# Delta-rule chunks of a two-block diffusion transformer: the identity of the Newton residual moves from TensorE's accumulation to VectorE's eviction, and the last chunk's directions are summed on VectorE

## The chip, the cores and the metric

The kernel runs on one core of a Trainium2 chip. A time is the device time of one execution in microseconds (us). A core has five instruction queues that run side by side and wait for each other through semaphores: PE (TensorE, matmuls; its weight loads are listed as PEld), DVE (VectorE), ACT (ScalarE), POOL (GpSimd) and SP (SyncE, here the queue that issues most transfers). Each queue runs its instructions strictly in the order in which the program has them. Matmuls write to PSUM, which is read by DVE and ACT; everything else lies in SBUF.

## The reference

One launch computes two transformer blocks on 512 tokens of width 1024. Block 1 has two recurrences side by side (HGRN2 and a gated delta rule, each with 4 heads of 128, in both directions of time, each started from a context of 256 tokens), an output projection and a mixture of 16 experts; block 2 has attention, a gating unit and two convolutional feed-forward layers. The change touches the delta rule:

```
a_mat = where(strict, beta * (k k^T) * decay, 0) + eye      # per chunk and head, unit lower triangular
sol   = triangular_solve(a_mat, [k*beta*exp(cum), v*beta])  # w, u
v_new = u - w @ state
o     = q_dec @ state + (q k^T * decay) @ v_new
state = g_tot * state + k_dec^T @ v_new
...
return oc_f + flip(oc_b), ox_f + flip(ox_b)                 # the two directions are summed
```

The kernel uses chunks of 128 tokens: 2 of the context and 4 of the sequence, in each of two directions, so 12 chunks.

## The kernel before, in words

The program is written with a tile library: pools of buffers, and one list of instructions in which waits are put in by the library, and in which the order on each engine is chosen by the library's scheduler when the program is built. So a changed instruction can move others.

Of the whole program the delta-rule core takes the stretch from about 472 to 690 us. `dn_core` makes 12 generators (`dn_chunk`, one for each chunk and direction) and `in_turn(chunks, 5, 3, fill)` runs them: up to five chunks are in flight, a new one enters every third turn, and each `yield` ends a chunk's turn. `fill` adds the steps of a matrix-vector product (block 2's modulation) while it lasts. I call three turns a round: one chunk enters and one leaves in each.

A chunk goes through these steps, all on tiles of 128 x 512 (4 heads side by side):

- lines 1035 to 1041: the decays, `r` and `a` (on GpSimd, in the context's chunks on VectorE), cumulated by matmuls, and `e`, their exponential, on ScalarE.
- lines 1051, 1052: `a *= e`, `a *= kk` on VectorE; then `a` is transposed into `at`, and half-precision inverses `xi` and `ti` are begun (1061 to 1066; the masked copy into `ti` is line 1065).
- lines 1067 to 1088: six levels of block doubling. Each multiplies `at` with `ti` into `y` (evicted by ScalarE, 1072), `y` with `xi` and `xi` with `y`, and copies both products under a mask into `xi` and `ti` (VectorE, 1086 and 1087; the last two levels copy blocks, 1029).
- lines 1089 to 1098: two Newton steps on the inverse, `xf += tb^T (I + a^T xf)`, where `a` is by then the negated matrix with its diagonal. The residual `I + a^T xf` is made in a PSUM bank, evicted as the bfloat16 tile `res`, and multiplied with `tb`; line 1098 adds the product to `xf` on VectorE. This is the place of the first edit.
- lines 1102 to 1146: the read-out matrix `qk`, `vb` (line 1117, VectorE, 4 small instructions), `vn`, the output `o` (ScalarE, 1132; VectorE, 1133) and the new state (VectorE, 1145). For the second direction to reach a chunk, `finish` is given: its output goes to `dnoc`, is added to the first direction's in `dno` (line 1135), and is normed and gated by `head_out` (ScalarE line 787, VectorE 305, GpSimd 306, VectorE 790). This is the place of the second edit.

PSUM gives the chunks a pool `mm` of 5 banks and a pool `aux` of 3.

After the core follows block 1's output projection: its weights come by SP (line 506) into `wraw` and `wrawx`, ScalarE rounds them into `whi` (line 270), VectorE takes the remainder `wlo` (line 273), the gated outputs are transposed on PE (650) and split into `hhi` and `hlo` in the same way, and three matmuls (530 to 532) make one product. `hosq` is the scratch tile of `head_out`'s squares.

Of the kernel before, what the change touches and what calls it, by code (L numbers as in the profile page):

```python
# [225 lines left out]
class Kern:  # L226
# [771 lines left out]
    def dn_chunk(self, pool, d, c, x, ab, s, po, finish=None, zero=False, last=False):  # L998
# [6 lines left out]
        nc = self.nc  # L1005
        inc, exc = self.incs[d], self.c["lt" if d else "gt"]
        d4 = slice(4 * d, 4 * d + 4)
        full, hb = [P, 4, P], lambda ap: ap.unsqueeze(2).to_broadcast([P, 4, P])
# [7 lines left out]
        def mm4(p, l, r, start=True, stop=True):  # L1016
            for h in range(4):
                nc.tensor.matmul(p[:, h, :], l[:, h, :], r[:, h, :], start=start, stop=stop)
# [13 lines left out]
        p = aux()  # L1032
# [7 lines left out]
        a = tile_("a")  # L1040
        eng.tensor_mul(a, exc.unsqueeze(1).to_broadcast(full), hb(ab["nbeta"][:, c, d4]))
        yield
        if ("kk", c) not in x:
            for n, l in (("kk", "kT"), ("qk", "qT")):
                if l in x:
                    p = mmt()
# [7 lines left out]
        p = aux()  # L1054
# [12 lines left out]
        for l in range(5, -1, -1):  # L1067
            yield
            p = aux()
# [7 lines left out]
            if l == 0:  # L1077
                xf, tb = tile_("xf"), tile_("tb", BF16)
# [9 lines left out]
        for i in range(2):  # L1088
            yield
            p = mmt()  # L1090
            nc.tensor.matmul(p, self.identb, self.identb.unsqueeze(1).to_broadcast(full), start=True, stop=False)
            for h in range(4):
                nc.tensor.matmul(p[:, h, :], a[:, h, :], xf[:, h, :], start=False, stop=h == 3)
            res = tile_("res", BF16)
            nc.scalar.copy(res, p)
            p = mmt()
            mm4(p, tb, res)
            nc.vector.tensor_add(xf, xf, p)

        yield  # L1100
        if po is not None:
            nc.gpsimd.tensor_mul(e, e, x["qk", c][d])
            p = aux()
# [9 lines left out]
        if not zero:  # L1113
            p = mmt()
# [5 lines left out]
        p = mmt()  # L1120
# [4 lines left out]
        if po is not None:  # L1125
            p = mmt()
            mm4(p, x["qT"][:, :, cs], s)
            p2 = mmt()
            mm4(p2, qk, vn)
            o = tile_("oc")  # L1130
            for h in range(4):
                nc.scalar.mul(o[:, h, :], p[:, h, :], ab["ec"][:, c, 4 * d + h:4 * d + h + 1])
            nc.vector.tensor_add(o if finish else po, o, p2)
            if finish:
                nc.gpsimd.tensor_add(po, po, o)
                finish()
        if last:
            return
        p = mmt()
# [974 lines left out]
```

## Time and profile before

| | |
|---|---|
| median of three runs | 2383.46 us (2381.67 to 2384.58) |
| the profiled execution | 2387.35 us |
| its span, first to last instruction | 2385.5 us |
| PE busy over the span | 94% |
| DVE busy | 68% |
| ACT busy | 50% |
| POOL busy | 26% |
| mean granted clock of TensorE | 0.972 of full speed |

The busy shares are means over stages with different limits. A stage is read from its own stretch of the trace.

### The profile page before, as it was taken

What the parts mean: (1) busy time and instruction counts of PE and PEld (TensorE: products, weight loads), DVE (VectorE), ACT (ScalarE), POOL (GpSimd) and SP (SyncE); (2) the same over time, 40 slices, a digit from 0 to 9 for tenths busy, and PEclk for the clock granted to TensorE, in tenths of its full rate; (3) what the DMA queues carried; (4) which work ended last, traced back from release to release, by engine and by line L of the source; (5) the groups of instructions that cost most, each with busy time, mean ns of one, the idle gap of its engine ahead of it and who ended that gap; (6) DMA issues with size and microseconds to landing.
All of it is one profiled execution on the core that took longest, in us unless ns stands there. A gap on an engine that the chain in (4) does not pass through costs nothing.

```text
span 2385.5 us, 33834 instructions
## 1 busy us (share of the span) xinstructions
PE 2240.5 (94%) x13058; PEld 1880.5 (79%) x13058; DVE 1614.3 (68%) x2545; ACT 1200.8 (50%) x1969; POOL 620.3 (26%) x470
## 2 busy tenths in 40 slices
PE   6998989989988899999999999999999999999998
PEld 3988977758875677778778878878888988888887
DVE  4777877778855888886857865896673445553553
ACT  4455644456754677776337763432342433432433
POOL 2133544345421111100441422332333001110111
PEclk9999999999999899999999999999999999999999
DMA  8564004151045799997210002656433222323321
GB/s 317 186 222 143 28 1 153 46 219 74 2 177 230 281 395 368 372 379 267 77 39 1 2 36 107 237 193 231 148 131 102 102 89 71 106 73 113 106 74 60
DMA packets 68405, 355.24 MB, mean 149 GB/s; under 512 B 8065, under 2 KB 12817, under 8 KB 37009
## 3 DMA queue, kind: packets, MB, share of 16 engines
q1 hardware_dynamic: 62752, 333.94, 38.0%
q0 software_dynamic: 5488, 19.11, 3.3%
q8 instruction: 104, 1.70, 0.3%
q14 instruction: 61, 0.49, 0.1%
HBM read 334.45 MB, written 19.40 MB: 148 GB/s over the span
## 4 chain that ended last, share of the span: by engine, by line
PE 43%; DVE 5%; issue 1%; ACT 1%; DMA 0%; POOL 0%; SPq 0%; POOLq 0%; DVEq 0%; ACTq 0%
PE mm L531 12%; PE mm L532 12%; PE mm L530 12%; PE sc L1598 2%; PE av L1751 1%; PE aux L1616 1%; DVE mva L385 1%; PE av L1742 1%; DVE smax L1605 1%; DVE wlo L273 1%; PE aux L1587 0%; DVE cy L1868 0%; PE aux L388 0%; DVE st L1577 0%; DVE alo L273 0%
## 5 line engine op out<-in xcount | busy, mean ns | idle before, releaser
L530 PE MATMUL mm<-hhi,whi 128*128 128x512 f32 (+1 forms) x1184 | 438.0, 375 | 10.3 <-ACT whi L270 5.3
L531 PE MATMUL mm<-hlo,whi 128*128 128x512 f32 (+1 forms) x1184 | 441.5, 374 | 2.9 <-DVE hlo L482 2.9
L532 PE MATMUL mm<-hhi,wlo 128*128 128x512 f32 (+1 forms) x1184 | 438.7, 372 | 0.0
L270 ACT CAST whi<-wraw 128x1024 fp32r<-128x1024 f32 (+1 forms) x240 | 246.3, 1041 | 300.1 <-PE mm L531 223.5
L273 DVE TENSOR_TENSOR wlo<-wraw,whi 128x1024 fp32r<-128x1024 f32 (+1 forms) x203 | 249.3, 1244 | 179.9 <-ACT whi L270 179.1
L273 DVE TENSOR_TENSOR wlo<-wrawx,whi 128x1024 fp32r<-128x1024 f32 x190 | 229.0, 1230 | 94.3 <-ACT whi L270 93.0
L270 ACT CAST whi<-wrawx 128x1024 fp32r<-128x1024 f32 (+1 forms) x210 | 215.0, 1048 | 154.2 <-PE mm L531 106.1
L530 PEld LDWEIGHTS mm<-hhi,whi 128*128 128x128 f32 x1184 | 224.8, 191 | 49.4 <-ACT whi L270 5.9
L531 PEld LDWEIGHTS mm<-hlo,whi 128*128 128x128 f32 x1184 | 225.9, 191 | 41.5 <-DVE hlo L482 3.3
L532 PEld LDWEIGHTS mm<-hhi,wlo 128*128 128x128 f32 x1184 | 225.4, 191 | 38.0 <-issue 0.2
L530 PE MATMUL mm<-whi,hhi 128*128 128x512 f32 (+1 forms) x640 | 218.2, 346 | 6.3 <-ACT hhi L481 2.3
L532 PE MATMUL mm<-whi,hlo 128*128 128x512 f32 (+1 forms) x640 | 219.9, 347 | 3.8 <-DVE hlo L482 3.7
L531 PE MATMUL mm<-wlo,hhi 128*128 128x512 f32 (+1 forms) x640 | 219.6, 345 | 0.5 <-DVE wlo L273 0.4
L385 DVE SCALAR_TENSOR_TENSOR mva<-mvr,cc_c,mva 128x512 f32<-128x512 f32 x154 | 156.6, 1017 | 3.4 <-DMA mvr<-in_w_mod_dram 1.2
L1878 POOL TENSOR_TENSOR cy<-cy,csg 128x512 f32<-128x512 f32 x44 | 64.7, 1472 | 348.0 <-DVE cy L1870 332.5
L531 PE MATMUL mm<-alo,whi 128*128 128x512 f32 (+1 forms) x396 | 145.0, 366 | 0.0
L530 PE MATMUL mm<-ahi,whi 128*128 128x512 f32 (+1 forms) x396 | 144.7, 367 | 0.0
L532 PE MATMUL mm<-ahi,wlo 128*128 128x512 f32 (+1 forms) x396 | 144.4, 366 | 0.0
L273 POOL TENSOR_TENSOR wlo<-wraw,whi 128x1024 fp32r<-128x1024 f32 (+1 forms) x37 | 90.1, 2434 | 203.7 <-ACT whi L270 195.4
L530 PEld LDWEIGHTS mm<-whi,hhi 128*128 128x128 f32 x640 | 125.1, 196 | 20.3 <-ACT hhi L481 2.8
L532 PEld LDWEIGHTS mm<-whi,hlo 128*128 128x128 f32 x640 | 124.9, 196 | 19.7 <-DVE hlo L482 6.2
L531 PEld LDWEIGHTS mm<-wlo,hhi 128*128 128x128 f32 x640 | 125.0, 196 | 14.4 <-DVE wlo L273 1.3
(548 smaller groups left out, 4672.4 us busy)
## 6 DMA issues: line engine op xcount, KB each, us to landing
wrawx<-in_w_down_dram SPq DMA_DIRECT2D x32, 1024.0 KB, 9.1
wrawx<-in_w_gate_dram SPq DMA_DIRECT2D x30, 1024.0 KB, 9.0
wraw<-in_w_up_dram SPq DMA_DIRECT2D x30, 1024.0 KB, 9.2
wraw<-in_ffn_w_up_dram SPq DMA_DIRECT2D x30, 1024.0 KB, 4.8
mvr<-in_ada_w_dram SPq DMA_DIRECT2D x56, 512.0 KB, 4.5
wraw<-in_ada_w_dram SPq DMA_DIRECT2D x20, 1024.0 KB, 4.9
wraw<-in_w_in_dram SPq DMA_DIRECT2D x18, 1024.0 KB, 6.9
mvr<-in_w_mod_dram SPq DMA_DIRECT2D x32, 512.0 KB, 4.4
```

Source lines behind the costliest of these rows:

```text
L270: nc.scalar.copy(hi, src)
L273: (lo_eng or nc.vector).tensor_sub(lo, src, hi.bitcast(F32))
L385: nc.vector.scalar_tensor_tensor(acc, raw[:, k, :], c, acc, op0=ALU.mult, op1=ALU.add)
L530: nc.tensor.matmul(out, ahi, bhi, start=start, stop=False)
L531: nc.tensor.matmul(out, ahi, blo, start=False, stop=False)
L532: nc.tensor.matmul(out, alo, bhi, start=False, stop=stop)
L1598: nc.tensor.matmul(s[:, a:a + n], qs[:, qt * P:qt * P + P], ks[i][:, a:a + n], start=i == 0, stop=i == 1)
L1605: nc.vector.tensor_reduce(m, s[:, :768], axis=AX.X, op=ALU.max, negate=True)
L1616: nc.tensor.transpose(tp[:, j, :], p[:, (a + j) * P:(a + j + 1) * P], self.ident)
L1742: nc.tensor.matmul(av[:, qt, :], pt[:, k, :], hd["v"][:, k, :], start=k == 0, stop=k == 5)
L1751: nc.tensor.matmul(av[j * 64:j * 64 + 64, qt, :], hd["v"][:, k, :], pt[:, k, :], start=k == 0, stop=k == 5, tile_position=(0, j * 64))
L1878: nc.gpsimd.tensor_mul(y, y, sg)
```

## The change

Two edits. First, the identity: before, a bfloat16 matmul of the identity with itself puts `I` into the bank, four single-precision matmuls accumulate `a^T xf` onto it, and ScalarE casts the bank to `res`. After, the four matmuls start the bank, and VectorE's `tensor_add` reads the bank and the float32 identity (a constant in SBUF, repeated for the 4 heads) and writes `res`. That happens twice in each of 12 chunks. Second, where a chunk is the last of its direction (`last`, i == 3, which is so for the last two chunks of the 12), line 1135's sum of the two directions runs on VectorE and not on GpSimd.

```diff
         for i in range(2):
             yield
             p = mmt()
-            nc.tensor.matmul(p, self.identb, self.identb.unsqueeze(1).to_broadcast(full), start=True, stop=False)
-            for h in range(4):
-                nc.tensor.matmul(p[:, h, :], a[:, h, :], xf[:, h, :], start=False, stop=h == 3)
+            mm4(p, a, xf)
             res = tile_("res", BF16)
-            nc.scalar.copy(res, p)
+            nc.vector.tensor_add(res, p, self.ident.unsqueeze(1).to_broadcast(full))
             p = mmt()
             mm4(p, tb, res)
             nc.vector.tensor_add(xf, xf, p)
...
             if finish:
-                nc.gpsimd.tensor_add(po, po, o)
+                (nc.vector if last else nc.gpsimd).tensor_add(po, po, o)
                 finish()
```

The scheduler answers by moving neighbours. In the changed program line 1095's eviction is line 1093, 1098 is 1096, 1117 is 1115, 1133 is 1131 and 1135 is 1133; elsewhere in this text lines are those of the kernel before.

VectorE, one round in the middle of the core, before (`dnxf` is `xf`, `dnkkc` the chunk's k k^T, `smask` the masks):

```order
L1117 SCALAR_TENSOR_TENSOR dnvb<-mm,dnt,dnvb 128x128 x4
L1098 TENSOR_TENSOR dnxf<-dnxf,mm 128x512
L1086 COPY_PREDICATED dnxi<-smask,mm 128x512
L1087 COPY_PREDICATED dnti<-smask,mm 128x512
L1051 TENSOR_TENSOR dna<-dna,dne 128x512
L1086 COPY_PREDICATED dnxi<-smask,mm 128x512
L1087 COPY_PREDICATED dnti<-smask,mm 128x512
L1052 TENSOR_TENSOR dna<-dna,dnkkc 128x512
L1098 TENSOR_TENSOR dnxf<-dnxf,mm 128x512
L1065 COPY_PREDICATED dnti<-smask,dna 128x512
```

The same stretch of VectorE after the change (`cst` is the constant that holds the identity):

```order
L1115 SCALAR_TENSOR_TENSOR dnvb<-mm,dnt,dnvb 128x128 x4
L1093 TENSOR_TENSOR dnres<-mm,cst 128x512
L1051 TENSOR_TENSOR dna<-dna,dne 128x512
L1096 TENSOR_TENSOR dnxf<-dnxf,mm 128x512
L1052 TENSOR_TENSOR dna<-dna,dnkkc 128x512
L1086 COPY_PREDICATED dnxi<-smask,mm 128x512
L1087 COPY_PREDICATED dnti<-smask,mm 128x512
L1086 COPY_PREDICATED dnxi<-smask,mm 128x512
L1087 COPY_PREDICATED dnti<-smask,mm 128x512
L1065 COPY_PREDICATED dnti<-smask,dna 128x512
L1093 TENSOR_TENSOR dnres<-mm,cst 128x512
L1096 TENSOR_TENSOR dnxf<-dnxf,mm 128x512
```

Two instructions more; lines 1051 and 1052 now stand ahead of the four masked copies, and the second residual behind them and behind line 1065.

ScalarE, the end of the core, before (from the last chunk's `vn` on):

```order
L1123 COPY dnvn<-mm 128x512
L787 ACTIVATE hosq,hoss<-dno 128x128
L270 CAST whi<-wraw 128x1024 x2
L787 ACTIVATE hosq,hoss<-dno 128x128 x2
L270 CAST hhi_7474<-aux 128x512 x3
L270 CAST whi<-wrawx 128x1024
```

The same place on ScalarE after the change:

```order
L1121 COPY dnvn<-mm 128x512
L787 ACTIVATE hosq,hoss<-dno 128x128
L270 CAST whi<-wraw 128x1024 x2
L787 ACTIVATE hosq,hoss<-dno 128x128
L270 CAST whi<-wrawx 128x1024 x2
L787 ACTIVATE hosq,hoss<-dno 128x128
L270 CAST hhi_7450<-aux 128x512 x3
```

Both casts of the weights in `wrawx` have moved ahead of the last chunk's first square and of the three casts `hhi` that the output projection's first matmuls read.

VectorE, the end of the core after the change, from the last chunk's output on:

```order
L1131 TENSOR_TENSOR dnoc<-dnoc,mm 128x512
L273 TENSOR_TENSOR wlo<-wraw,whi 128x1024
L1133 TENSOR_TENSOR dno<-dno,dnoc 128x512
L273 TENSOR_TENSOR wlo<-wraw,whi 128x1024
L305 TENSOR_SCALAR hoss<-hoss 128x4
L1417 MEMSET pbase 128x16
L1423 CAST tw<-cst 128x64
L1433 MEMSET ofl 128x16
L273 TENSOR_TENSOR wlo<-wrawx,whi 128x1024 x2
L790 SCALAR_TENSOR_TENSOR oxd<-dno,hoss,oxd 128x128 x4
L273 TENSOR_TENSOR hlo_7451<-aux,hhi_7450 128x512 x3
```

The sum of the directions has come in between the two `wlo`; before, the three `hlo` stood directly behind line 1435's memset (1433 here), ahead of line 790 and of the two `wlo` of `wrawx`.

## Rows read from the trace of the kernel before

**Rows 1.** The page: engines' busy time, then one of the costliest groups.
```profile
PE 2240.5 (94%) x13058; PEld 1880.5 (79%) x13058; DVE 1614.3 (68%) x2545; ACT 1200.8 (50%) x1969; POOL 620.3 (26%) x470
...
L385 DVE SCALAR_TENSOR_TENSOR mva<-mvr,cc_c,mva 128x512 f32<-128x512 f32 x154 | 156.6, 1017 | 3.4 <-DMA mvr<-in_w_mod_dram 1.2
```

**Rows 2.** Busy us by stretch: length, PE, PEld, DVE, ACT, POOL, clock, DMA.
```profile
507.00:523.00 16.00, 13.30 (x152) 9.58 (x149) 12.16 (x25) 10.60 (x21) 5.62 (x5) 1.00 0.57 223
...
603.06:617.82 14.76, 13.75 (x152) 12.57 (x152) 13.55 (x28) 10.29 (x23) 8.38 (x7) 1.00 0.01 2
...
646.74:659.35 12.61, 11.77 (x138) 10.90 (x136) 10.06 (x24) 9.57 (x25) 2.31 (x2) 1.00 0.00 1
...
700.00:720.00 20.00, 20.00 (x104) 16.89 (x103) 11.27 (x14) 11.55 (x20) 7.54 (x7) 1.00 0.73 291
```

**Rows 3.** Timeline of DVE, one round: start, us, instruction, idle before and its ender.
```profile
595.83 0.93 DVE L1065 CAST_PREDICATED dnti<-smask,dna 128x512 f16<-128x512 uint8 x1
...
599.09 0.69 DVE L1133 TENSOR_TENSOR dno<-dnoc,mm 128x512 f32<-128x512 f32 x1 [0.52 <-ACT dnoc L1132]
...
604.73 0.69 DVE L1098 TENSOR_TENSOR dnxf<-dnxf,mm 128x512 f32<-128x512 f32 x1 [0.55 <-PE mm L1018]
...
608.33 1.56 DVE L1052 TENSOR_TENSOR dna<-dna,dnkkc 128x512 f32<-128x512 f32 x1
609.81 0.68 DVE L1098 TENSOR_TENSOR dnxf<-dnxf,mm 128x512 f32<-128x512 f32 x1
610.41 0.93 DVE L1065 CAST_PREDICATED dnti<-smask,dna 128x512 f16<-128x512 uint8 x1
```

**Rows 4.** Timeline of POOL in the round of rows 3.
```profile
608.08 1.26 POOL L1102 TENSOR_TENSOR dne<-dne,dnqkc 128x512 f32<-128x512 f32 x1
609.30 1.48 POOL L1041 TENSOR_TENSOR dna<-cst,dnnb 128x512 f32<-128x512 f32 x1
```

**Rows 5.** Groups of DVE's instructions by form, 559 to 648 us.
```profile
L1052 DVE TENSOR_TENSOR dna<-dna,dnkkc 128x512 f32<-128x512 f32 x6 | 7.6, 1271 | 1.0 <-ACT dnkkc L1050 1.0
...
L1065 DVE CAST_PREDICATED dnti<-smask,dna 128x512 f16<-128x512 uint8 x6 | 6.9, 1143 | 0.1
```

**Rows 6.** Timeline of PE and ACT at the round's two residuals.
```profile
602.00 0.38 PE L1091 MATMUL mm<-identb 128*128 128x512 bf16 x1
...
602.22 1.05 PE L1093 MATMUL mm<-dnxf,dna 128*128 128x128 f32 x8
...
604.30 0.39 PE L1018 MATMUL mm<-dnres,dntb 128*128 128x128 bf16 x4
...
604.75 0.63 ACT L1039 ACTIVATE dne<-aux 128x512 f32<-128x512 f32 x1
...
607.77 0.59 ACT L1095 CAST dnres<-mm 128x512 bf16<-128x512 f32 x1 [0.52 <-PE mm L1093]
...
608.41 0.38 PE L1018 MATMUL mm<-dnres,dntb 128*128 128x128 bf16 x4 [0.45 <-ACT dnres L1095]
```

**Rows 7.** Timeline of all engines at the end of the core.
```profile
684.81 2.01 ACT L270 CAST whi<-wraw 128x1024 fp32r<-128x1024 f32 x2
...
686.59 3.42 DVE L273 TENSOR_TENSOR wlo<-wraw,whi 128x1024 fp32r<-128x1024 f32 x2
...
686.75 2.18 POOL L1135 TENSOR_TENSOR dno<-dno,dnoc 128x512 f32<-128x512 f32 x1 [4.49 <-DVE dnoc L1133]
...
688.96 0.31 ACT L787 ACTIVATE hosq<-dno 128x128 f32<-128x128 f32 x1 [1.84 <-POOL dno L1135]
...
689.27 1.54 ACT L270 CAST hhi<-aux 128x512 fp32r<-128x512 f32 x3
...
689.94 1.19 PE L530 MATMUL mm<-hhi,whi 128*128 128x512 f32 x2 [4.09 <-POOL zero L2021]
```

**Rows 8.** The load of `wrawx` there: us to landing, then its issue on SP.
```profile
wrawx<-in_w_out_dram SPq DMA_DIRECT2D x1, 1024.0 KB, 4.6
...
684.23 0.33 SPq L506 DMA_DIRECT2D wrawx<-in_w_out_dram  x1
```

## The prediction

> **What bounds the kernel now.** I began with the page's busy shares: over the span PE is busy 94% and DVE 68% [rows 1], which would say that DVE has room. That is a mean over stages, and the edits touch one of them, so I went to busy time by stretch. In a round in the middle of the core (603.06 to 617.82) PE is busy 13.75 of 14.76 us and DVE 13.55, ACT 10.29 and POOL 8.38 [rows 2]: two engines are nearly full, and which of them sets the pace is not told by shares. The timeline of DVE tells it [rows 3]. From one start of line 1065 (595.83) to the next (610.41) a round takes 14.58 us, and DVE stands idle in it at two places only: 0.52 us before line 1133, where ScalarE's product is late, and 0.55 us before the first line 1098, where the residual comes back from ACT and PE. The rest runs without a gap, a full-size instruction every 0.60 us (609.81 to 610.41) though each row shows 0.68.
>
> Two rows of that round are longer than their kind: line 1052 with 1.56 and line 1065 with 0.93. Both read two SBUF tiles, and in both a POOL instruction is under way: line 1102 ends at 608.08 + 1.26 = 609.34 and line 1052 at 609.89, one instruction's length later; line 1041, which follows on POOL, is stretched over that time to 1.48 [rows 3, 4]. So DVE's SBUF-only instructions and POOL's wait for each other. Line 1098, which has one operand in PSUM, ran 0.68 beside line 1041 unhindered [rows 3, 4]. The six instances from 559 to 648 average 1271 ns (line 1052) and 1143 ns (line 1065) [rows 5], so this is no accident of one round, and there are six such rounds.
>
> The ledger of DVE's round is then: waits 0.52 + 0.55 = 1.07; waits for POOL (1.56 - 0.68) + (0.93 - 0.68) = 1.13; work 14.58 - 1.07 - 1.13 = 12.38.
>
> **The first edit, in the six full rounds.** PE loses the identity's matmul: the next one starts 0.22 us after it (602.00, 602.22) [rows 6], so 0.22 twice a round. ACT loses two casts of 0.59 [rows 6]. DVE gains two evictions. The trace shows no `tensor_add` of a PSUM bank and a constant with bfloat16 output; the nearest row is line 1098, also one PSUM and one SBUF operand of 128 x 512, with 0.68 and a slot of 0.60 [rows 3]. I take 0.60. Work becomes 12.38 + 1.20 = 13.58.
>
> What remains of the waits? The 0.52 before line 1133 stays, since its chain over PE and ACT isn't touched. In the new order the second residual and its line 1098 are neighbours, and between them lies a trip to PE: 0.05 from the end of `res` to the matmul (607.77 + 0.59 = 608.36, 608.41) and 0.43 from the matmul to line 1098 (604.30, 604.73) [rows 3, 6], 0.48 us with nothing to do; before, that trip was hidden, since line 1098 came behind line 1052. At the first residual line 1051 fills the trip, but line 1051 needs `e`, which ACT finished at 604.75 + 0.63 = 605.38 [rows 6], while DVE would come to it at 604.18 + 0.60 = 604.78 (604.18 is where the wait of 0.55 began). With PE 0.22 and ACT up to 0.59 earlier, `e` is 0 to 0.5 late: 0.25. Together 1.25.
>
> So a round takes 13.58 + 1.25 = 14.83 if POOL never hinders: 0.25 more than now. With the 1.13 of now it takes 15.96, 1.38 more. If lines 1051, 1052 and 1065 each meet a POOL instruction as badly as line 1052 did (0.88), it takes 14.83 + 2.64 = 17.47, 2.89 more; line 1051 now stands where POOL makes the next `r`, so this can be. POOL's work doesn't change, so I take the middle value, 1.4. The cause shows on PE as a late second product: its matmul waits behind four masked copies, line 1065 and the eviction, where ACT answered 0.52 us after it had become free [rows 6]. PE itself, with 13.75 - 0.44 us, no longer sets the pace. Six rounds: 8.4 us, bounds 1.5 and 17.3.
>
> The Trainium skill speaks against this edit (Perfetto Trace Analysis, "Optimizing Scalar/DVE Operations"): what both engines can do may go from a saturated DVE to ScalarE; here it goes the other way. The same section puts the overhead of an access to PSUM at about 125 ns on DVE and 51 ns on ScalarE; an estimate from it makes each of 24 residuals 0.074 us slower by itself, 1.8 us in all. The rows of the two instructions, 0.68 and 0.59 [rows 3, 6], make it 0.09 and 2.2 us. Either is small beside the queueing.
>
> **The other six rounds.** The three at the head are not DVE's: 12.16 of 16 us busy, beside transfers and a matrix-vector product on PE [rows 2]. There an eviction falls into idle time; PE saves 0.44 a round, and each residual is 0.68 - 0.59 = 0.09 slower. I put these rounds at 0, bounds -1.3 (all of PE's saving) and +1.5. In the three at the tail DVE is 80% busy or less (10.06 of 12.61) [rows 2], room for 1.2; the chain itself is longer by 6 x 0.09. I put 0.6, bounds 0 and 2.4 (two rounds that pay 1.2).
>
> **The second edit.** Now the last sum takes POOL 2.18 us (686.75 to 688.93), beside DVE's two `wlo`, both SBUF-only, and ACT's square waits 1.84 us for it; `hhi` follows at 689.27 and PE starts the output projection at 689.94 after 4.09 us of idle [rows 7]. With a DVE sum of 0.68 directly behind line 1133 the square could start at about 687.3, 1.65 earlier. But the order of ACT has changed: two casts of `wrawx` now stand ahead of that square and of `hhi`. Their load is issued at 684.23 and lands 4.6 us later [rows 8], at 688.83. Behind the cast that waits for it stand the square and `hhi`, and PE waits for `hhi`. Two casts at 2.01 / 2 = 1.0 each [rows 7] end at 690.85, the square takes 0.31, `hhi` starts at 691.2, and PE 0.67 later at 691.85: 1.9 us later than before. Behind that, VectorE's `hlo` now stands behind the `wlo` of `wrawx` and line 790, which can hold PE's next products for up to 2 us more. I take 3, bounds -1.65 (as the edit alone would have it) and +4. The last but one sum has nobody behind it that waits on the path. From there the delay goes on in full: the output projection keeps PE busy 20.00 of 20 us [rows 2].
>
> Later stages get the same instructions in a slightly other order (for example loads of the matrix-vector products among the feed-forward weights). Nothing prices it; those products' DVE groups waited 1.2 us in all for a load [rows 1], so I put 0.
>
> **The sum.** 8.4 + 0 + 0.6 + 3 = 12.0 us. Against the profiled execution's own 2387.35 us (span 2385.5 and 1.85 around it) that is 2399.4; this execution lay 3.9 above the median of the three runs, 2383.46, so the median should be **2395.5 us**.
>
> **The rivals.** A change of 0.2%, 4.8 us, is about what a measurement of this kernel can tell from none.
>
> - *DVE full, as summed* (more than 4.8 us slower, up to about 2400): chance 0.66.
> - *POOL meets every one of the three moved or lengthened instructions*: 17.3 + 0.6 + 3 = 20.9, 2404.4 us. For it: by the code line 1051 now comes up just as POOL, freed by the cumulating matmuls, makes the next `r`. Against: over six rounds, whose orders differ, lines 1052 and 1065 lost (1271 - 680) + (1143 - 680) = 1054 ns together [rows 5], about one meeting a round. The Trainium skill (SBUF — State Buffer, "SBUF: two separate sides") describes such a pair of ports, shared by the two engines, as a lock that the first comer holds for its whole instruction; the 609.34 and 609.89 above agree. Chance 0.11.
> - *Absorbed*: the new places of lines 1051, 1052 and 1065 happen to miss POOL, so that 0.25 a round remains, 1.5 in all, and the end comes out even: 1.5 + 0.6 = 2.1, 2385.6 us. For it: POOL is idle 6 of 14.76 us [rows 2]. Chance 0.16.
> - *Faster: PE sets the pace*. Then 24 x 0.22 = 5.3 us go, and 1.65 at the end: 7.0, 2376.5 us. For it: PE is the busiest engine even in the full rounds [rows 2], and DVE does wait for PE in them. It decides once DVE's waits of both kinds fall under 14.58 - 0.44 - 13.58 = 0.56 us a round, where they are 2.20 now; the trip behind the second residual alone is 0.48. Chance 0.07.
>
> **How the numbers follow.** The first two cases are slower by over 0.2%: 0.77; absorbed is the same, 0.16; faster 0.07. The range goes from the absorbed case's side, 2384, with the small losses in it, to 2406, a little over the second case; it leaves out the faster case and the lowest part of absorbed, with some 0.05 above. The likeliest case by itself spans 2388 to 2401.
>
> **What would show it.** Right: in the middle of the core a round of about 16 us; DVE without a gap but for 0.5 before line 1133 and 0.5 between the second residual and line 1098; PE idle before the product with `res` for over 1 us, where it was 0.45 [rows 6]; rows of lines 1051, 1052 or 1065 well over 0.68. At the end ACT casting `wrawx` before `hhi`, and PE's idle time about 6 us instead of 4.09. Wrong: rounds of 14.6 us or less; new evictions of line 1093 far from 0.68; or a stage after the core that starts no later relative to the last `vn`.

## The result, and the profile after

The changed kernel takes 2403.7 us (median of 5 runs, 2398.8 to 2410.21) against 2383.46 (2377.88 to 2389.99): 20.2 us more. The ratio over all executions is 1.0091 (of the two medians alone 1.0085), with a 95% interval of 1.0074 to 1.0108. It is slower, by more than the 12 us forecast. Its profiled execution takes 2403.28 us, span 2401.5, which is 16.0 above the span of the profile before. From here on a line has the number of the kernel in which it is shown; besides those given with the change, 1102 of before is 1100 in the changed kernel, and 1132 is 1130.

The page's busy times answer to [rows 1], and say no more than those did:

```profile
PE 2237.8 (93%) x13034; PEld 1878.0 (78%) x13034; DVE 1629.1 (68%) x2571; ACT 1192.1 (50%) x1945; POOL 616.9 (26%) x468
```

Busy time by stretch, changed kernel, a round in the middle of the core and a round in the tail (columns as in [rows 2]):

```profile
605.94:623.22 17.28, 14.97 (x152) 13.87 (x149) 15.19 (x30) 9.45 (x21) 7.70 (x7) 0.90 0.01 1
655.78:668.92 13.14, 11.47 (x136) 10.83 (x134) 11.10 (x25) 8.64 (x23) 2.31 (x2) 1.00 0.01 2
```

The round has grown from 14.76 to 17.28 us, DVE is busy 1.64 longer in it, ACT 0.84 less; the round in the tail has grown from 12.61 to 13.14. The timeline of DVE in that round, beside [rows 3]:

```profile
605.94 1.12 DVE L1115 SCALAR_TENSOR_TENSOR dnvb<-mm,dnt,dnvb 128x128 f32<-128x128 f32 x4
606.98 0.68 DVE L1093 TENSOR_TENSOR dnres<-mm,cst 128x512 bf16<-128x512 f32 x1
607.94 1.40 DVE L1051 TENSOR_TENSOR dna<-dna,dne 128x512 f32<-128x512 f32 x1 [0.28 <-ACT dne L1039]
609.26 0.67 DVE L1096 TENSOR_TENSOR dnxf<-dnxf,mm 128x512 f32<-128x512 f32 x1
609.86 1.37 DVE L1052 TENSOR_TENSOR dna<-dna,dnkkc 128x512 f32<-128x512 f32 x1
...
613.55 0.68 DVE L1065 CAST_PREDICATED dnti<-smask,dna 128x512 f16<-128x512 uint8 x1
614.15 0.68 DVE L1093 TENSOR_TENSOR dnres<-mm,cst 128x512 bf16<-128x512 f32 x1
615.80 0.69 DVE L1096 TENSOR_TENSOR dnxf<-dnxf,mm 128x512 f32<-128x512 f32 x1 [0.97 <-PE mm L1018]
...
619.14 0.69 DVE L1131 TENSOR_TENSOR dno<-dnoc,mm 128x512 f32<-128x512 f32 x1 [0.71 <-ACT dnoc L1130]
```

Between them, POOL (beside [rows 4]):

```profile
607.75 1.04 POOL L1035 TENSOR_TENSOR dnr<-cst,dnlah 128x512 fp32r<-128x512 f32 x1
609.42 1.27 POOL L1100 TENSOR_TENSOR dne<-dne,dnqkc 128x512 f32<-128x512 f32 x1 [0.62 <-DVE dna L1051]
...
614.04 1.08 POOL L1041 TENSOR_TENSOR dna<-cst,dnnb 128x512 f32<-128x512 f32 x1 [1.77 <-PE mm L1018]
```

Two of DVE's rows last twice their kind: line 1051 ends 0.55 after POOL's `r` (607.75 + 1.04 = 608.79; 609.34), line 1052 0.54 after POOL's line 1100 (610.69; 611.23). The groups over the six rounds, changed kernel, beside [rows 5]; and line 1051 in the kernel before:

```profile
L1093 DVE TENSOR_TENSOR dnres<-mm,cst 128x512 bf16<-128x512 f32 x12 | 8.2, 680 | 0.0
L1065 DVE CAST_PREDICATED dnti<-smask,dna 128x512 f16<-128x512 uint8 x6 | 7.3, 1219 | 0.1
...
L1052 DVE TENSOR_TENSOR dna<-dna,dnkkc 128x512 f32<-128x512 f32 x6 | 6.9, 1149 | 0.4 <-ACT dnkkc L1050 0.4
...
L1051 DVE TENSOR_TENSOR dna<-dna,dne 128x512 f32<-128x512 f32 x6 | 6.3, 1055 | 1.2 <-ACT dne L1039 0.8 <-POOL dnr L1035 0.3
```
```profile
L1051 DVE TENSOR_TENSOR dna<-dna,dne 128x512 f32<-128x512 f32 x6 | 4.1, 685 | 0.0
```

The residual lasts 680 ns, as line 1098 did. Line 1051 has gone from 685 to 1055 ns, line 1052 from 1271 to 1149, line 1065 from 1143 to 1219: meetings with POOL cost 0.32 us a round more than before.

At the end of the core (beside [rows 7, 8]), ACT, DVE, PE and SP of the changed kernel:

```profile
694.34 0.33 SPq L506 DMA_DIRECT2D wrawx<-in_w_out_dram  x1
...
697.79 0.69 DVE L1133 TENSOR_TENSOR dno<-dno,dnoc 128x512 f32<-128x512 f32 x1
...
699.00 2.00 ACT L270 CAST whi<-wrawx 128x1024 fp32r<-128x1024 f32 x2 [1.77 <-DMA wrawx<-in_w_out_dram]
...
700.90 0.31 ACT L787 ACTIVATE hosq<-dno 128x128 f32<-128x128 f32 x1
...
701.21 1.54 ACT L270 CAST hhi<-aux 128x512 fp32r<-128x512 f32 x3
...
701.87 2.05 PE L530 MATMUL mm<-hhi,whi 128*128 128x512 f32 x4 [5.92 <-ACT hhi L270]
...
704.92 0.78 PE L531 MATMUL mm<-hlo,whi 128*128 128x512 f32 x1
```

The sum is done at 698.48, and the square that needs it starts at 700.90: between them stand the two casts that wait for `wrawx`. PE waits 5.92 us where it waited 4.09.

From starts of instructions I cut each profile into stretches (line numbers here are those of the kernel before). *Head*: first instruction of line 1035 on DVE to the first line 1117. *Six rounds*: from there to the seventh line 1117 of chunks. *Tail*: to the last line 1133 that adds to `dnoc`. *End*: to the first matmul of line 531. *Feed-forward*: the last score matmul (line 1598) to the first matmul of line 1828. *Over* is the median less that of before in the same runs. All in us:

| kernel | over | head | six rounds | tail | end | feed-forward |
|---|---|---|---|---|---|---|
| before | 0 | 87.30 | 88.34 | 39.25 | 5.64 | 516.1 |
| changed | 20.2 | 86.85 | 99.01 | 40.27 | 8.87 | 518.4 |
| e1 first edit alone | 14.3 | 88.16 | 99.02 | 40.25 | 5.65 | 514.6 |
| e2 second edit alone | 8.8 | 87.46 | 88.30 | 39.27 | 9.16 | 520.3 |
| e3 identity on PE, cast on VectorE | 14.4 | 88.74 | 97.94 | 40.29 | 5.64 | 512.5 |
| e4 identity left out, cast on ScalarE | 4.3 | 85.25 | 86.68 | 38.55 | 5.64 | 520.0 |
| e5 changed, block copies on ScalarE | 24.8 | 89.15 | 101.80 | 39.86 | 9.15 | 520.3 |
| e6 before, block copies on ScalarE | 1.2 | 87.88 | 88.82 | 39.19 | 5.64 | 512.5 |
| e7 changed, without `e *= qk` | 14.3 | 87.73 | 94.14 | 40.26 | 9.16 | 519.9 |
| e8 second edit, `hhi` first | 5.1 | 87.23 | 88.33 | 39.27 | 5.95 | 519.3 |
| e9 first residual only | 17.4 | 86.94 | 95.11 | 40.51 | 5.65 | 520.1 |
| e10 second residual only | 9.1 | 87.42 | 94.29 | 39.09 | 5.64 | 514.7 |
| e11 changed, line 1052 on GpSimd | 22.5 | 93.58 | 92.97 | 40.24 | 8.90 | 519.0 |
| e12 before, line 1052 on GpSimd | 5.0 | 92.62 | 86.46 | 39.28 | 5.64 | 514.6 |

The stretches of the core repeat to some hundredths where two programs have the same order there (six rounds 99.01 and 99.02; 88.34, 88.30 and 88.33; end 5.64 and 5.65), so a difference in them can be read from single profiles. The head varies by 1 to 2 us. The medians are less sure: they come from 5 to 23 executions, which differ by up to 13 us, and the stretches from one. With the feed-forward stage at the mean of its order (see e2), the medians lie between 2.0 us under (e7) and 4.2 us over (e9) what the stretches add up to. So the readings below rest on the stretches; a difference of a few us between medians shows little by itself.

### The profile page after: what moved, and what is told of

It is laid out like the page before. It is cut to its first block, busy times and chain, and to the rows that moved or that the text cites. A ratio compares the mean times of both kernels' runs of the same rounds, so it can differ in the third digit from the quotient of the medians.

```text
span 2401.5 us, 33788 instructions
## 1 busy us (share of the span) xinstructions
PE 2237.8 (93%) x13034; PEld 1878.0 (78%) x13034; DVE 1629.1 (68%) x2571; ACT 1192.1 (50%) x1945; POOL 616.9 (26%) x468
```

## The experiments

My theory after the comparison: VectorE sets the pace of the six rounds, so its load is the cost; the second edit pays at the end and in the later stages by what it reorders. The first four kernels take the two edits, and the two halves of the first, apart.

**e1**, the changed kernel without the second edit:

```diff
-                (nc.vector if last else nc.gpsimd).tensor_add(po, po, o)
+                nc.gpsimd.tensor_add(po, po, o)
```

> The first edit alone; the last sum stays on GpSimd. The program then has the end of the core and the later load order of the kernel before, and the core's order of the changed kernel. Theory (VectorE sets the pace of the six full rounds, and the second edit pays at the end and in the later stages by its reordering): the six rounds from the fifth to the eleventh line 1115 cost 10 to 11 us more than before (some 16.5 us each), nothing is added behind the core, so 11 us over before in the median, 2393 to 2396 us. Rival (the rounds grow because of something that comes with the second edit's reordering, or VectorE's eviction is absorbed when that is gone): under 5 us over before.

Measured: 14.3 over (ratio 1.0061, 1.0045 to 1.0078). Six rounds 10.7 longer, the end as before, the feed-forward stage not longer. The theory's place is right; the median of 2397.5 is 1.5 above its range, and the stretches account for 12.5 of the 14.3.

**e2**, the kernel before with the second edit:

```diff
-                nc.gpsimd.tensor_add(po, po, o)
+                (nc.vector if last else nc.gpsimd).tensor_add(po, po, o)
```

> The second edit alone; the residual is as before. The order behind the core is that of the changed kernel: both casts of wrawx ahead of hhi, and the later loads in the changed order. Theory: the core's rounds stay at 14.7 us; PE's restart is 1.9 us later relative to the last line 1133 than before, 3 us by the first matmul of line 531; another 2 to 2.5 us are lost in the feed-forward stage, where matrix-vector products have other places; 5 to 6 us over before, about 2389 us. Rival (the sum itself is quicker on VectorE, and the later stages absorb the reordering): 0 to 2 us under before.

Measured: 8.8 over (1.0043, 1.0029 to 1.0057), more than the theory's 5 to 6; the rival is out. The core is untouched, the end is 3.5 longer, and the feed-forward stage 4.2. That stage, e1 and then e2, in busy time by stretch:

```profile
1425.10:1939.70 514.60, 505.51 (x2591) 427.59 (x2590) 327.36 (x428) 194.63 (x269) 146.23 (x77) 0.99 0.44 151
```
```profile
1415.70:1936.00 520.30, 507.32 (x2591) 428.40 (x2590) 326.88 (x428) 195.11 (x269) 144.42 (x77) 0.99 0.43 149
```

The same instructions, but PE is idle 13.0 us in e2 and 9.1 in e1. SP has the loads of the matrix-vector products (`mvr`) at other places among the weights, and VectorE and PE have the products there at other places too. By the loads on SP there all programs have one of two orders. With that of before (before, e1, e3, e6, e10, e12) the stage takes 512.5 to 516.1 us, mean 514.2; with that of the changed kernel (the other eight, called the new order below) 518.4 to 520.3, mean 519.7. The new order goes with 5.5 us, more than the 2.3 that the first two profiles show, of which before's is the longest of its group.

The traces show where most of it lies. PE's wait for VectorE's finished product, again e1 and then e2 (us, times, longest), and a stretch of e2:

```profile
PE aux L388 <- DVE mva L385: 4.6, 4, 1.6
```
```profile
PE aux L388 <- DVE mva L385: 8.4, 7, 2.2
```
```profile
1638.00:1641.00 3.00, 3.00 (x8) 2.33 (x8) 2.93 (x6) 0.00 (x0) 0.00 (x0) 0.50 0.93 334
```

Over the two groups this wait averages 4.7 and 8.2 us, so 3.5 of the 5.5 are PE waiting for line 385. The other 2 are PE's busy time, at a mean clock of 0.988 against 0.992. Both groups have stretches at a granted 0.50 behind other waits of this stage, in some executions and not in others; but one more, just behind a wait of 2.0 to 2.2 us before line 388, is in all eight programs of the new order and in none of the old (there the longest such wait is 1.6). That the new order brings it is likely, and was not tested apart; nor was which instruction's place makes line 385 late.

**e3**, the kernel before with the cast alone moved:

```diff
-            nc.scalar.copy(res, p)
+            nc.vector.tensor_copy(res, p)
```

> The kernel before, with the identity's matmul kept on PE and only the cast of the residual moved from ScalarE to VectorE. Theory (VectorE's load is the cost, PE's matmul of the identity is hidden): rounds as in the changed kernel, 16.0 to 16.6 us, and 9 to 12 us over before, the same as with the first edit alone within 2 us. Rival (PE's 0.22 us twice a round are on the path too, and the first edit gains them back): 2.5 to 5 us more than with the first edit alone, 14 to 16 us over before.

Measured: 14.4 over (1.0068, 1.0054 to 1.0082). That lies above the theory's 9 to 12 and inside the rival's 14 to 16, but so does e1's 14.3, and the rival turns on the difference to e1. Medians are too rough to tell 2.5 to 5 us apart; the stretches can: head, six rounds and tail together are 0.5 us shorter than e1's, where the rival wants them 2.5 to 5 us longer. PE's identity matmul is hidden once VectorE evicts, and the eviction is the cost.

**e4**, neither identity nor sum:

```diff
-            nc.tensor.matmul(p, self.identb, self.identb.unsqueeze(1).to_broadcast(full), start=True, stop=False)
-            for h in range(4):
-                nc.tensor.matmul(p[:, h, :], a[:, h, :], xf[:, h, :], start=False, stop=h == 3)
+            mm4(p, a, xf)
             res = tile_("res", BF16)
             nc.scalar.copy(res, p)
```

> The identity is left out altogether (neither matmul nor sum, so the Newton step lacks its identity), ScalarE casts as before, the last sum stays on GpSimd. PE's saving is there without VectorE's load. The order behind the core is before's at the core's end, and the changed kernel's in the later loads. Theory: PE does not set the pace; only the wait of 0.55 us ahead of the first line 1096 shortens by 0.22 us, rounds of 14.3 to 14.6 us, 1 to 2 us less over the six; the later order costs 2 to 2.5 us: between 0 and 2 us over before. Rival (PE sets the pace once VectorE's load is not raised): 0.44 us less a round in all twelve, 5 us under before, 2.5 with the later order.

Measured: 4.3 over (1.0024, 1.0014 to 1.0035), worse than both. In the core PE's saving comes back: six rounds 1.7 shorter, as the theory has it, head 2.1, tail 0.7, together 4.4 of 24 x 0.22 = 5.3. The median is over before all the same; this program has the new order behind the core, 5.5 us in the feed-forward stage, which leaves 3.2 of the 4.3 unexplained. So in the core what the first edit saves on PE is worth having while ScalarE evicts, and nothing (e3) once VectorE does.

The next two ask whether it is VectorE's load as such. **e5** (on the changed kernel) and **e6** (on the one before) move three small copies a round to ScalarE:

```diff
-                (nc.scalar.copy if n else nc.vector.tensor_copy)(dst[rows, :, cols], p[rows, :, cols])
+                nc.scalar.copy(dst[rows, :, cols], p[rows, :, cols])
```

> The changed kernel, with the last two levels' block copies of xi (line 1029, three small instructions a round on VectorE: 0.46 + 2 x 0.31 = 1.07 us) moved to ScalarE; the residual stays where it is on VectorE. Theory (VectorE's occupation sets the round): rounds shorter by about 1.07 us, 15.4 instead of 16.5, six rounds by 6.4, in all 6 to 8 us under the changed kernel, 2396 to 2398 us. Rival (the residual's place in VectorE's queue and its trips through PE set the round, not VectorE's load): rounds within 0.3 us of 16.5, or longer since the copies now wait in ScalarE's queue; 2402 to 2406 us.

> The kernel before, with the same block copies moved from VectorE to ScalarE, and nothing else. Theory (VectorE sets the pace already before, with PE close behind at 13.75 us of 14.76): rounds of 13.9 to 14.3 us, 3 to 5 us less over six, about 2379 us, and a loss behind the core only if the later loads change place. Rival (before, PE and its chain over ScalarE set the pace): rounds within 0.2 us of 14.7, 2382 to 2385 us, or longer as line 1133's wait for ScalarE grows.

Measured: e5 24.8 over before (1.0103, 1.0085 to 1.012), 4.6 more than the changed kernel's; six rounds 2.8 longer, not 6.4 shorter. e6 1.2 over (1.0004, 0.9992 to 1.0015). **Here the theory in its plain form fell**: 1.07 us less on VectorE did not shorten the six rounds of either kernel. In e5, groups of DVE over the six rounds:

```profile
L1131 DVE TENSOR_TENSOR dno<-dnoc,mm 128x512 f32<-128x512 f32 x4 | 2.8, 688 | 6.8 <-ACT dnoc L1130 6.8
```

DVE waits 6.8 us in four rounds for ScalarE's `dnoc`, where it waited 3.1 in the changed kernel:

```profile
L1131 DVE TENSOR_TENSOR dno<-dnoc,mm 128x512 f32<-128x512 f32 x4 | 2.7, 686 | 3.1 <-ACT dnoc L1130 3.1
```

The copies now stand in ScalarE's queue ahead of it. The Trainium skill (Perfetto Trace Analysis, "Optimizing Scalar/DVE Operations") says that giving work of a saturated DVE to ScalarE may make sense. By busy shares this was such a case (DVE 15.19 of 17.28 us, ACT 9.45), and here it did not pay. These two runs relieve VectorE and load ScalarE at once, so they do not show what the relief alone would have given.

So the theory became: from line 1115 to the second residual VectorE's own line of instructions sets the round; behind the second line 1096 the round goes through ScalarE as well. Work taken off the first part should count, work moved from the second to ScalarE not.

**e7**, the changed kernel without POOL's line 1100:

```diff
-            nc.gpsimd.tensor_mul(e, e, x["qk", c][d])
```

> The changed kernel, with GpSimd's product of the decays and q k^T (line 1100, e *= qk) left out, so that the read-out takes the bare decays. In the changed kernel line 1052 lasts 1.37 us while line 1100 is under way on GpSimd, and line 1051 lasts 1.40 while line 1035 is. Theory (VectorE's instructions with two SBUF operands wait for GpSimd's): line 1052 falls to 0.68 in these rounds and line 1051 stays as it is; rounds 0.4 to 0.6 us shorter, six rounds by 2.5 to 3.5, 2400 us. Rival (the length comes from something else, as operands or PSUM): line 1052 keeps 1.3 us, rounds as they are, 2403 us.

Measured: 14.3 over before (1.0053, 1.0035 to 1.0072), 5.9 less than the changed kernel's. DVE's groups over the six rounds of e7:

```profile
L1051 DVE TENSOR_TENSOR dna<-dna,dne 128x512 f32<-128x512 f32 x6 | 6.5, 1076 | 0.9 <-POOL dnr L1035 0.6 <-ACT dne L1039 0.2
L1065 DVE CAST_PREDICATED dnti<-smask,dna 128x512 f16<-128x512 uint8 x6 | 5.6, 933 | 0.1
...
L1052 DVE TENSOR_TENSOR dna<-dna,dnkkc 128x512 f32<-128x512 f32 x6 | 4.1, 685 | 0.4 <-ACT dnkkc L1050 0.3
```

Line 1052 falls from 1149 to 685 ns, line 1065 from 1219 to 933, line 1051, which meets another instruction of POOL, stays. That is (0.46 + 0.29) x 6 = 4.5 us; the six rounds give back 4.9. The lengthening is GpSimd's doing, and in this part of the round it counts in full. The Trainium skill (SBUF — State Buffer, "SBUF: two separate sides") names the cause, a port pair that the first comer keeps for its whole instruction. This run agrees: 1149 ns beside line 1100, 685 without it.

**e8**, the second edit with an order edge:

```diff
+                with ExitStack() as behind:
+                    if b == 4 and not done:
+                        behind.enter_context(self.tc.issue_after(third))
-                lead += [(b + kp, m, whi, wlo) for kp, m, whi, wlo in self.unit(w.rows(b), 0, 4, [(0, 256)])]
+                    lead += [(b + kp, m, whi, wlo) for kp, m, whi, wlo in self.unit(w.rows(b), 0, 4, [(0, 256)])]
```

(`third` is the third `hhi` cast, `b` the block of 128 rows.)

> The second edit alone, with ScalarE's two casts of wrawx held behind the first three casts hhi by an order edge. Theory (at the end PE waits for hhi, which stands behind the casts that wait for the load): PE restarts 2.3 us after the start of the last line 1133, where it was 3.95 before and 6.11 with the second edit alone; the first matmul of line 531 follows within 2 us; what the later loads' changed order costs stays, so 2384 to 2389 us, 3 to 5 us under the second edit alone. Rival (PE waits for something else there, as the transposes or VectorE's hlo): PE's first product with line 531 starts no earlier than in the second edit alone, 9.2 us after the last line 1133.

Measured: 5.1 over (1.0024, 1.0015 to 1.0033), 3.7 under e2, and what is left is about the 5.5 of the new order. PE restarts 3.58 us after line 1133's start, not 2.3 as expected, and line 531 follows at 5.95. Line 1133 of the kernel before, and then DVE, ACT and PE at the end of the core in e8 (line 1138 is 1133 of before, 1140 its 1135, 795 its 790, 653 its 650):

```profile
685.99 0.69 DVE L1133 TENSOR_TENSOR dnoc<-dnoc,mm 128x512 f32<-128x512 f32 x1 [4.02 <-ACT whi L270]
```
```profile
684.36 0.69 DVE L1138 TENSOR_TENSOR dnoc<-dnoc,mm 128x512 f32<-128x512 f32 x1 [3.43 <-ACT whi L270]
...
684.96 1.22 DVE L273 TENSOR_TENSOR wlo<-wraw,whi 128x1024 fp32r<-128x1024 f32 x1
...
686.17 0.68 DVE L1140 TENSOR_TENSOR dno<-dno,dnoc 128x512 f32<-128x512 f32 x1
...
687.28 1.54 ACT L270 CAST hhi<-aux 128x512 fp32r<-128x512 f32 x3
...
687.75 1.14 DVE L795 SCALAR_TENSOR_TENSOR oxd<-dno,hoss,oxd 128x128 f32<-128x128 f32 x4 [0.63 <-POOL hoss L306]
...
687.94 1.19 PE L530 MATMUL mm<-hhi,whi 128*128 128x512 f32 x2 [3.68 <-ACT hhi L270]
...
688.81 1.88 DVE L273 TENSOR_TENSOR hlo<-aux,hhi 128x512 fp32r<-128x512 f32 x3
...
689.55 1.12 PE L653 MATMUL aux<-cst,oxh 128*128 128x128 f32 x4 [0.41 <-DVE hlo L273]
```

So the casts ahead of `hhi` were what held PE: without them it restarts 2.5 us earlier than in e2 (6.11). (The edge also moves the second cast of `wraw` behind `hhi`; that one had been done before the wait.) But the sum does not stand directly behind line 1133: a `wlo` of 1.22 us lies between, so it ends 2.49 us after line 1133's start, where POOL's in the kernel before ended after 2.94 (688.93 - 685.99), and PE then waits for `hlo`, which stands behind line 795. With the order mended the end is 0.3 us longer than before: in this order the second edit gives nothing.

**e9** and **e10** give the new form to one of the two residuals each, on the kernel before:

```diff
             res = tile_("res", BF16)
+            if i == 0:
+                mm4(p, a, xf)
+                nc.vector.tensor_add(res, p, self.ident.unsqueeze(1).to_broadcast(full))
+            else:
...
```

(`i == 1` in e10.)

> Only the first of a chunk's two residuals has the new form; the second keeps identity matmul and ScalarE's cast. After the block copies showed that work taken from VectorE behind the second line 1096 does not shorten a round, the theory is this: from line 1115 to the second residual VectorE's own line of instructions sets the round, behind that ScalarE and VectorE wait for each other. Then this half costs its 0.68 us and the longer line 1051, less the wait of 0.55 us that it fills: rounds of 15.0 to 15.5 us, 3 to 5 us over six. Rival (only the second residual costs, by its trip and its queue): rounds within 0.3 us of 14.7.

> Only the second residual has the new form; the scheduler puts it between lines 1052 and 1065, so that its trip through PE lies behind line 1065. The loads behind the core are in the order of the kernel before. Theory: 0.6 us a round on VectorE's line, nothing for the trip: rounds of 15.2 to 15.6 us, 3.5 to 5.5 us over six and the same in the median. Rival (the cost of the change hangs on the first residual, with the moved lines 1051 and 1052): rounds within 0.3 us of 14.7.

Measured: e9 17.4 over (1.0065, 1.0048 to 1.0082), six rounds 6.8 longer; e10 9.1 over (1.0033, 1.0021 to 1.0045), six rounds 6.0 longer. Both halves cost, each more than was forecast, so neither rival holds. (Of e10's 6.0 some 1.4 may be a fall of PE's clock; see the last section.) Together they are 12.8, more than the 10.7 of both at once: the halves do not add. e9 has the new order behind the core, e10 the old one, which is 5.5 of the 8.3 between their medians; about 4 of e9's 17.4 us and 3 of e10's 9.1 are in no stretch of the table and stay unexplained.

**e11** (on the changed kernel) and **e12** (on the one before) take work off the first part:

```diff
-        nc.vector.tensor_mul(a, a, x["kk", c][0])
+        nc.gpsimd.tensor_mul(a, a, x["kk", c][0])
```

> The changed kernel, with line 1052 (a *= kk), which lasts 1.37 us on VectorE in the six rounds, moved to GpSimd. It is work ahead of the second residual. Theory (in that part of the round VectorE's line sets the pace): rounds shorter by 0.9 to 1.3 us, 15.2 to 15.6, six rounds by 5.5 to 8, 2396 to 2398 us. Rival (as with the block copies: work taken from VectorE comes back as a wait): rounds within 0.3 us of 16.5 or longer.

> The kernel before, with line 1052 moved to GpSimd, where it took 1.56 us on VectorE in the middle of the core. Theory (VectorE's line ahead of the second residual sets the pace, PE is close behind with 13.75 us): rounds of 13.9 to 14.3 us, six rounds 3 to 5 us shorter, 2379 to 2381 us unless the later loads take it back. Rival (PE and ScalarE set the pace in the kernel before): rounds within 0.3 us of 14.7, 2383 to 2386 us.

Measured: e11 22.5 over before (1.0084, 1.0067 to 1.0101); its six rounds are 6.0 shorter than the changed kernel's, as the theory has it. That is lost again in the head, 6.7 us longer: there line 1052 stands in GpSimd's queue behind `gate_weight`'s product and its load. DVE in e11's head:

```profile
499.97 0.69 DVE L1065 CAST_PREDICATED dnti<-smask,dna 128x512 f16<-128x512 uint8 x1 [7.34 <-POOL dna L1052]
```

e12 5.0 over (1.0012, 1.0000 to 1.0023): head 5.3 longer in the same way, six rounds only 1.9 shorter, not 3 to 5. Its line 1065 now meets GpSimd:

```profile
L1065 DVE CAST_PREDICATED dnti<-smask,dna 128x512 f16<-128x512 uint8 x6 | 9.0, 1494 | 0.0
```

(1143 ns before, [rows 5].) No kernel of these beats the one before. Moving line 1052 in the sequence's chunks alone might spare the head and, as an estimate from e12's six rounds, gain 1.9 us; it was not tried.

## Why the prediction was right, and which of its terms were too small

The sign, the place and the mechanism were right: the rounds in the middle of the core carry the loss, VectorE is where it arises, and PE's saving is hidden. Of the 20 us the first edit brings 11.2 (six rounds, head and tail) and the second 8.7 (the end, and the new order behind the core, which e2 has and e1 has not; in e4 and e9 the scheduler takes it without the second edit). Two terms were too small.

*Six rounds, 8.4 forecast, 10.7 measured.* The forecast round had 1.20 us more work, 0.18 more waiting and the meetings with POOL as they were. Of the eviction's slot, I took 0.60; the twelve take 0.68 each (8.2 us), since in eleven of the twelve places DVE waits for something behind them and nothing overlaps with their ends (606.98 to 607.94 less 0.28; 614.15 to 615.80 less 0.97): 0.16 a round. DVE's waits over the six rounds sum to 8.6 us, 7.5 before: 0.17 a round, as forecast. The meetings grew by 0.32 a round: line 1051, moved to where POOL makes `r`, meets it, which I had named and given to the rival of 0.11; it went about a fifth of the way there (0.32 of 2.64 - 1.13). So 1.38 + 0.16 + 0.32 = 1.86 a round, against (99.01 - 88.34) / 6 = 1.78.

*Later stages, 0 forecast, 5.5 measured.* I put 0 because the `mva` groups waited only 1.2 us for their loads; "nothing prices it" was no reason for nothing, and it was the wrong wait: PE waits for the finished product, 3.5 us longer in the new order. Eight programs with the new order against six with the old one price it now.

*End, 3 forecast, 3.2 measured*: the two casts ahead of `hhi` (1.87 of the 1.9 forecast) and the `hlo` behind them. Here every step was as written. The lower bound, -1.65, was out of reach: by e8 the sum does not stand directly behind line 1133.

*Head 0 and tail 0.6 forecast*: -0.45 (and 0.86 in e1, with the same order) and 1.0.

Together 10.7 + 5.5 + 3.2 - 0.45 + 1.0 = 20.0, against 20.2 measured; that this fits to 0.2 is luck, since the same sum misses other runs by up to 4. Taking 3.9 off for the profiled execution was right: medians of 14 and of 23 more executions are 2383.2 to 2384.3, and its feed-forward stage alone lies 1.9 above the mean of its order.

*The range held in part by luck.* 2403.7 lies outside the 2388 to 2401 of the likeliest case. It is inside the range because the upper end was set by the rival *POOL meets every one*, and it comes within 1 us of that rival's 2404.4. But the rival's cause is not what made up the difference: it wanted 17.3 us in the six rounds, they took 10.7, and the meetings account for 1.9 of that. The largest missing piece, 5.5 us behind the core, was in no case.

*The ledger's reading* was half right. It counted all of DVE's waits and work as one line that sets the round. From line 1115 to the second residual this holds (e7, and e11's six rounds); behind it, by e5 and e6, ScalarE counts too. Both evictions lie in the first part, so the sum came out near. The rival *faster* fails by the rounds themselves and by e3, *absorbed* by e1. The sign foreseen on PE, over 1 us of idle time before the product with `res`, did not come: it is 0.87 at most, and in the round shown above 0.57 before the first product and none before the second. PE's idle time is spread, with 1.00 before the product with `vb` and 0.74 before the next residual's matmul; over the six rounds it is 15.5 us, 5.5 before.

## What to carry to other kernels

Before moving work between two busy engines, find in the timeline for each part of the loop which engine's line runs without a gap there; the share over the round does not tell it, and work moved off in another part can come back as a wait. When an edit makes a scheduler reorder work far behind it, that order needs a price of its own, and several programs that share it give one. An engine that gets a moved instruction also gets its queue: ask what stands ahead of it in every phase, not only in the one that is to gain.

## What the runs showed of the hardware that was not expected

PE's granted clock fell to half in one of the six rounds of the changed kernel, which it did in none of the kernel before (1.00 in every round). By microsecond it is 0.50, the 1.2 GHz level, from 612 to 615; just before, PE had been idle for 1.00 and, after 1.16 us of matmuls, for 0.74 us. PE in the changed kernel:

```profile
607.72 0.38 PE L1018 MATMUL mm<-dnres,dntb 128*128 128x128 bf16 x4 [0.57 <-DVE dnres L1093]
...
609.99 1.16 PE L1018 MATMUL mm<-dnvb,dnxf 128*128 128x128 f32 x8 [1.00 <-DVE dnxf L1096]
611.89 2.07 PE L1018 MATMUL mm<-dnxf,dna 128*128 128x128 f32 x8 [0.74 <-DVE dnxi L1086]
```

Now e1, which has the same order there and kept the full clock: the same matmuls, then POOL's line 1041, then DVE from line 1065 on:

```profile
612.93 1.16 PE L1018 MATMUL mm<-dnvb,dnxf 128*128 128x128 f32 x8 [1.00 <-DVE dnxf L1096]
614.82 1.16 PE L1018 MATMUL mm<-dnxf,dna 128*128 128x128 f32 x8 [0.74 <-DVE dnxi L1086]
```
```profile
616.06 1.04 POOL L1041 TENSOR_TENSOR dna<-cst,dnnb 128x512 f32<-128x512 f32 x1 [0.86 <-PE mm L1018]
```
```profile
616.48 1.17 DVE L1065 CAST_PREDICATED dnti<-smask,dna 128x512 f16<-128x512 uint8 x1
...
618.74 0.69 DVE L1096 TENSOR_TENSOR dnxf<-dnxf,mm 128x512 f32<-128x512 f32 x1 [0.49 <-PE mm L1018]
```

Both rounds last 17.28 us, but not because the fall was free. With the slower matmuls DVE waits 0.97 us before the second line 1096, 0.48 longer than in e1. But POOL's line 1041 waits for PE too and starts 0.9 us later in the round, so that line 1065, which meets it in e1 and takes 1.17 us, takes 0.68. In this round the loss and the missed meeting cancel.

In e10 one round had a mean clock of 0.90 too, and it lasted 16.86 us where the rounds beside it lasted 15.35 and 15.49: there the same fall may have cost 1.4 us, which would put e10's six rounds at 4.5 over before, within what was expected of them. No second execution of e10 shows that round at the full clock, so this stays open.
